# The low-rank product inside the mixer's first block, both gate turns ahead of the third output unit, three plain units first in the output's second half

## The chip, the cores and the metric

The kernel runs on one core of a Trainium2 chip. The metric is the device time of one execution in microseconds (us); several runs are taken and the median counts. Beside them one execution was profiled, which gives the span, the trace and the page of the profile.

## The reference

One encoder layer on 256 tokens of width 2048, in float32:

```python
x = x + 0.5 * swiglu(rms_norm(x, ffn1_norm), ffn1_w_gate, ffn1_w_up, ffn1_w_down)
h = rms_norm(x, mix_norm)
u, q, k, v, g, a_lr = split(h @ w_in)              # pool 1024 | q 512 | k 512 | v 1024 | gate 1024 | low rank 16
y_pool = pool_mixer(u, pool_w, pool_scale)          # trailing means over 2/4/8/16 frames, per-group map
log_a = log_sigmoid(a_lr @ gla_w_a2 + gla_b_a) / 16 # diagonal forget gate of the linear attention
y_gla = gated_linear_attention(q, k, v, log_a) * silu(g)   # 4 heads, chunks of 64 frames, per-head norm
x = x + concat(y_pool, y_gla) @ w_out
x = x + cross_attention(rms_norm(x, xattn_norm), rms_norm(mem, mem_norm))   # 256 memory tokens
x = x + 0.5 * swiglu(rms_norm(x, ffn2_norm), ffn2_w_gate, ffn2_w_up, ffn2_w_down)
out = rms_norm(x, final_norm)
```

The change concerns the projection `w_in` with the low-rank forget gate, the output gate, and the product with `w_out`.

## The kernel before

Every weight is streamed from memory once, in units of 1 MB: two 128-row slices of the weight by 1024 columns. A float32 product is made of three products of a reduced format. Each operand is split into a high part and a low part; high times high, high times low and low times high are added in PSUM. So each unit of raw weights is first split: ScalarE copies it to `wh` (the high part, L1671) and VectorE subtracts to get `wl` (the low part, L453).

A **plain** unit is 24 matmuls of 128x512 (L362). Some units go by a scheme of Strassen's kind and are called **sevens** here (L507): 7 products in place of 8, so 21 matmuls, for which VectorE forms sums of the weights (`T`, L486), and three weight blocks are split unsummed (`xh` L279, `xl` L280), the four sums as `wh` (L489) and `wl` (L453). The activations of a seven need sums as well (`Sums.make`, L424 to L436, and the `ye` tiles).

PSUM holds four tiles of two banks each. A block of eight units (`block_s`) uses two tiles (the **whole** tiles) for all units, and two more (the **parts** tiles) from its first seven on. After its last seven, `combine` (L581 to L586) reads the parts tiles, and after its last unit `join` (L596) or the residual (L767, L779) reads the whole tiles.

The order of the work comes from three things. `Stream` is a list of units and of small operations that are hung behind them: `st.op(f, n)` puts `f` behind the n-th unit that follows. When unit u is reached, the split of unit u+2 is written down first, then the matmuls of u, and the load of a further unit is issued into one of three raw buffers. If the next entry of the list is marked as a clump, the split of the low part is shared: GpSimd takes 768 of its 2048 columns (L457). A planner then orders each engine's queue by that program order and by its own estimate of when things are ready. Two means pin the order: `issue_after` puts instructions of one engine behind a named one in its queue, and `in_turn` and `among_weights` chain the splits of the weights (and the sums of activations) on VectorE and ScalarE in the order in which they were written down.

The mixer runs these blocks of eight units, each over the same activations `xs`, in the order of `ORDER_IN = (0, 2, 4, 1, 5, 3, 6, 7)` with units 1 and 3 as sevens:

- the **q/k block** (columns from 2·NB), whose rows are turned to columns by `turn_qk(1)` and `turn_qk(0)` (transposes at L789, copies at L1145);
- the **low-rank unit** (`load_a`, `a_unit`, `split_a`; L1056, L1065, L1072): one load of 16 columns, 16 matmuls into `pa`, read by `ev_a` (L1081 to L1083), which makes `aT`;
- the **pool block** (columns from 0). Inside its first unit, between its two halves, `decay_logits` (L1088 to L1096) multiplies `aT` with `wa2`; two units in, `decay` (L1096 to L1126) makes the cumulative sums of the forget gate, with three loads of activation tables. `decay` pins its logarithm behind the splits already written down, and pins the split that follows behind its subtraction (L1114);
- the **value block** and the **gate block**, with the attention of the four heads and the small pool product (L1044) between their units.

`gate(1)` and `gate(0)` turn the scaled gate rows by eight transposes each (L789), multiply them into the heads' outputs (L1253) and split them into `ys` (L285, L286). They are hung behind the first unit of the output block.

The **output block** is `into_x(w_out)` with the plan `MIXED`: its first half (1024 columns) takes the units in the order (1, 2, 3, 6, 0, 5, 4, 7) with 0 and 4 as sevens, its second half in the order (1, 2, 0, 3, 4, 5, 6, 7) with 0, 4 and 6 as sevens. `MIXED.after = (1, 4, 9)` says behind how many units of the block the sums of the activation pairs 0, 4 and 6 are made. `behind` pins the whole third unit (index 2) of the first half behind the transposes of `gate(1)` in TensorE's queue. Each half ends in four residual updates and two folds: `fold` transposes the new x (`px`, L800, 16 transposes for both) and scales it into `xs` (ScalarE L248, VectorE L240), which frees the two PSUM tiles of `px`. The query block of the cross attention follows.

Of the kernel before, what the change touches and what calls it, by code (L numbers as in the profile page):

```python
# [20 lines left out]
NB = 512  # L21
# [78 lines left out]
def build(ctx, tc, I, out):  # L100
    nc = tc.nc
    st = Stream()
# [87 lines left out]
    xs = main.tile([P, KT, 2, S], F32R, tag="xs", name="xs")  # L190
# [74 lines left out]
    def behind_weights(f):  # L265

        with tc.issue_after(latest["vector"].ins), tc.issue_after(latest["scalar"].ins):
            return f()
# [366 lines left out]
    def wload(dst, w, k0, n, n0, cols=NB):  # L635
        nc.sync.dma_start(
            dst, w[k0 * P : (k0 + n) * P, n0 : n0 + cols].rearrange("(k p) n -> p k n", p=P)
        )
# [9 lines left out]
    def wwide(w, n0, k0=0, nk=KT):  # L648

        def src(k):  # L650
            def load(raw):
                raw = raw.rearrange("p (k n) -> p k n", n=2 * NB)
                if len(loaded) < 3:
                    for kk in range(2):
                        parts = (0, NB) if not loaded else (0,)
                        for c in parts:
                            n = 2 * NB // len(parts)
                            wload(raw[:, kk : kk + 1, c : c + n], w, k + kk, 1, n0 + c, n)
                else:
                    wload(raw, w, k, 2, n0, 2 * NB)  # L660
                next(first_loads, None)
                loaded.append(1)
            return load
        return [src(k0 + k) for k in range(0, nk, 2)]
# [146 lines left out]
    class IntoX:  # L811
# [7 lines left out]
        def make_sums(self, after=None):  # L819
            for g, n in zip(self.sums.pairs, after or self.after):  # L820
# [1 line left out]

    WHOLE = IntoX((0, 4), (2, 5), ((1, 2, 3, 5, 0, 6, 4, 7), (1, 2, 0, 3, 4, 5, 6, 7)),
                  ((0, 4), (0, 4)))
    MIXED = IntoX((0, 4, 6), (1, 4, 9), ((1, 2, 3, 6, 0, 5, 4, 7), (1, 2, 0, 3, 4, 5, 6, 7)),
                  ((0, 4), (0, 4, 6)), room=3, folds=(1, 1, 2, 2))
    OUTPUT = IntoX((0, 4, 6), (0, 4, 9), ((1, 2, 3, 5, 0, 6, 4, 7), (1, 2, 0, 3, 4, 5, 6, 7)),
                   ((0, 4), (0, 4, 6)), room=3, folds=(1, 1, 2, 2))
# [3 lines left out]
    def into_x(w, act, scale, gain=None, k0=0, nk=KT, spread_too=True, src=None, way=OUTPUT,  # L832
               spread_at=3, behind=None):

        for b in range(2):
            st.op(lambda b=b: fetch_x(b, src), 2)
            cols = wwide(w, b * 2 * NB, k0, nk)
            if way.sevens[b]:
                block_s(cols, act, way.sums, way.orders[b], residual(scale, b, 0),
                        early_parts(scale, b), way.sevens[b], behind=None if b else behind)  # L840
            else:
                block_t(cols, act, residual(scale, b))
            if gain is not None:
                for j in range(2):
                    st.op(lambda c=2 * b + j: fold(c, gain), way.folds[2 * b + j])
        if gain is not None:
            st.op(lambda: finish_norm(4, spread_too), way.folds[3] + 1)
            if spread_too:
                st.op(spread_norm, spread_at)
# [94 lines left out]
    def in_ys(i):  # L944
        t = ys[:, 2 * i : 2 * i + 2].rearrange("p k a s -> p (k a s)")
        return t.rearrange("p (a n s) -> p a n s", a=2, n=4)

    qk_sums = Sums("qe", xs, (1, 3), False, 2, {0: in_ys(6), 1: in_ys(7)})
# [16 lines left out]
    w_in = I["w_in"][0]  # L965
    mix = {}
# [172 lines left out]
    def turn_qk(j):  # L1139
        if "kq" not in mix:  # L1140
            mt("kq", [P, 4 * LINES])
        t = mix["k" if j else "q"] = mix["kq"][:, j * H * S : (j + 1) * H * S].rearrange(
            "p (h s) -> p h s", h=H
        )
        nc.scalar.copy(t, rows_turned(mix["rows", j]))  # L1145
# [29 lines left out]
    def queries(h):  # L1175
        q, E, F = mix["q"][:, h, :], mix["E"], mix["F"]
        e = lambda c: E[:, 4 * h + c : 4 * h + c + 1]
        f = lambda i: F[:, i, h : h + 1]
        QD = mix["QD", h] = m4()
        at = QD_AT  # L1180
        factors = {(0, 1): e(1), (0, 2): f(0), (0, 3): f(2), (1, 2): e(2), (1, 3): f(1), (2, 3): e(3)}
        for j in range(3):
            nc.scalar.copy(QD[:, at[j] + j * CH : at[j] + (j + 1) * CH], q[:, j * CH : (j + 1) * CH])
            for c in range(j + 1, 4):
                nc.vector.tensor_scalar_mul(
                    QD[:, at[j] + c * CH : at[j] + (c + 1) * CH], q[:, c * CH : (c + 1) * CH],
                    factors[j, c],
                )

    def scores(h):  # L1190
        q, kd, QD, at = mix["q"][:, h, :], mix["k"][:, h, :], mix["QD", h], QD_AT
        ps = ptile(uid("pq"))
        for j in range(4):
            part = slice((j % 2) * CH, (j % 2 + 1) * CH)
            rhs = QD[:, at[j] + j * CH : at[j] + S] if j < 3 else q[:, 3 * CH :]
            nc.tensor.matmul(
                ps[part, j // 2, j * CH : S], kd[:, j * CH : (j + 1) * CH], rhs, start=True, stop=True
            )
        s = score_tile(h)
        for j in range(4):  # L1200
            part = slice((j % 2) * CH, (j % 2 + 1) * CH)
            nc.scalar.copy(s[part, j // 2, j * CH :], ps[part, j // 2, j * CH : S])
# [56 lines left out]

    ORDER_IN = (0, 2, 4, 1, 5, 3, 6, 7)  # L1260
    st.op(query_rows, 3)
    block_s(wwide(w_in, 2 * NB), xs, qk_sums, ORDER_IN, ev_qk, home=wide_home)
    st.op(lambda: turn_qk(1), 1)
    st.op(lambda: turn_qk(0), 2)
    st.unit(load_a, a_unit, split_a)
    st.op(ev_a)
    st.op(decay, 2)
    def head(h):
        attend(h)
# [2 lines left out]
    def scores_of(*hs):  # L1272
        for h in hs:
            st.op(lambda h=h: scores(h))

    def queries_of(*hs):
        for h in hs:
            st.op(lambda h=h: behind_weights(lambda: queries(h)))

    block_s(wwide(w_in, 0), xs, qk_sums, ORDER_IN, ev_pool, home=wide_home,  # L1280
            behind={0: (0, decay_logits)}, amid={4: lambda: queries_of(0, 1), 6: lambda: scores_of(0, 1)})
    for f, h, after in (
        (queries, 2, 1), (scores, 2, 1), (queries, 3, 1), (scores, 3, 1), (lambda _: turn_pool(), None, 2),
        (means, 1, 3), (means, 2, 4), (means, 3, 7), (means, 0, 8),
# [23 lines left out]
    def homes(of):  # L1308
        return lambda: scope.update(shared={tag: list(of[tag]) for tag in of})
# [27 lines left out]
    def mem_fold(c):  # L1337

        v = four(ptile(uid("tm")))
        for j in range(4):  # L1340
# [6 lines left out]

    MIXED.make_sums()
    into_x(I["w_out"][0], ys, 1.0, G_X, spread_too=False, way=MIXED,
           behind={2: (1, lambda: mix["turned", 1])})  # L1350
    st.op(homes(Q_HOMES))
    st.op(mem_in, 2)
    for c in range(4):
# [337 lines left out]
def program(shapes):  # L1691
    import concourse.bacc as _bacc

    nc = _bacc.Bacc("TRN2", target_bir_lowering=False, num_devices=1)
    args = {
        name: nc.dram_tensor(f"in_{name}", shapes[name], F32, kind="ExternalInput").ap()
        for name in _INS
    }
    out = nc.dram_tensor("out", _OUT, F32, kind="ExternalOutput").ap()
    with tile.TileContext(nc, schedule_with_timeline_sim=True) as tc, ExitStack() as ctx:  # L1700
        build(ctx, tc, args, out)
    return nc
# [10 lines left out]
```

## Time and profile before

| | |
|---|---|
| median of 3 runs | 2077.58 us (2077.37 to 2078.93) |
| the profiled execution's own time | 2078.92 us |
| its span | 2077.1 us (the other 1.8 us lie around the span) |
| TensorE (PE) busy, matmuls | 2061.7 us (99%) |
| VectorE (DVE) busy | 1838.8 us (89%) |
| ScalarE (ACT) busy | 1171.3 us (56%) |
| granted TensorE clock | 0.999 |
| moved by the DMA engines | 435.92 MB, mean 210 GB/s |

In the trace the q/k block's last unit begins at about 747 us, the low-rank unit at 752.8, the pool block at 756.4, the output block at 906.2 and its second half at about 951; the query block follows at about 997. A row of the timeline has the start, the duration, the engine, the line, what is written from what, how often, and in brackets the idle time of the engine before it with what ended it.

### The profile page before, as it was taken

What the parts mean: (1) busy time and instruction counts of PE and PEld (TensorE: products, weight loads), DVE (VectorE), ACT (ScalarE), POOL (GpSimd) and SP (SyncE); (2) the same over time, 40 slices, a digit from 0 to 9 for tenths busy, and PEclk for the clock granted to TensorE, in tenths of its full rate; (3) what the DMA queues carried; (4) which work ended last, traced back from release to release, by engine and by line L of the source; (5) the groups of instructions that cost most, each with busy time, mean ns of one, the idle gap of its engine ahead of it and who ended that gap; (6) DMA issues with size and microseconds to landing.
All of it is one profiled execution on the core that took longest, in us unless ns stands there. A gap on an engine that the chain in (4) does not pass through costs nothing.

```text
span 2077.1 us, 24042 instructions
## 1 busy us (share of the span) xinstructions
PE 2061.7 (99%) x9461; PEld 1713.8 (83%) x9461; DVE 1838.8 (89%) x1717; ACT 1171.3 (56%) x1190; POOL 107.5 (5%) x95
## 2 busy tenths in 40 slices
PE   9999999999999999999999999999999999999998
PEld 7888888888888887887888888888888888888886
DVE  6998899989998769889889878889988999889987
ACT  7665455554554656566755554556554555545554
POOL 0000000000000000000000000000000010000001
PEclk9999999999999999999999999999999999999999
DMA  7666766566666655457755455666576765776664
GB/s 264 203 202 223 243 210 217 184 229 235 226 198 222 234 175 183 164 197 227 266 183 196 166 183 182 203 213 216 178 243 213 236 210 192 224 241 223 207 226 155
DMA packets 122985, 435.92 MB, mean 210 GB/s; under 512 B 9844, under 2 KB 13528, under 8 KB 122488
## 3 DMA queue, kind: packets, MB, share of 16 engines
q1 hardware_dynamic: 122696, 433.86, 62.4%
q8 instruction: 74, 1.21, 0.2%
q10 hardware_dynamic: 176, 0.53, 0.1%
q14 instruction: 39, 0.32, 0.0%
HBM read 417.58 MB, written 16.78 MB: 209 GB/s over the span
## 4 chain that ended last, share of the span: by engine, by line
PE 97%; DVE 1%; ACT 1%; DMA 0%; issue 0%; SPq 0%; DVEq 0%; ACTq 0%
PE pt L362 63%; PE pt L507 29%; PE ph L789 1%; PE pl L1396 1%; PE pv L1433 1%; DVE wl L453 1%; PE px L800 0%; DMA x<-in_x 0%; PE pp L1044 0%; PE pe L362 0%; DVE T L486 0%; ACT wh L489 0%; PE pa L1072 0%; PE tm L1342 0%; PE po L1209 0%
## 5 line engine op out<-in xcount | busy, mean ns | idle before, releaser
L362 PE MATMUL pt<-wh,xs 128*128 128x512 f32 x2464 | 790.2, 391 | 0.2 <-ACT wh L279 0.2
L1671 ACT CAST wh<-raw 128x2048 fp32r<-128x2048 f32 x243 | 463.8, 1913 | 224.7 <-PE pt L362 123.7
L453 DVE TENSOR_TENSOR wl<-raw,wh 128x2048 fp32r<-128x2048 f32 (+1 forms) x243 | 516.6, 2134 | 83.1 <-ACT wh L1671 82.8
L362 PEld LDWEIGHTS pt<-wh,xs 128*128 128x128 f32 x2464 | 461.8, 188 | 95.8 <-ACT wh L279 0.6
L489 ACT CAST wh<-T 128x1024 fp32r<-128x1024 f32 x262 | 274.8, 1053 | 380.4 <-DVE T L486 367.5
L362 PE MATMUL pt<-wl,xs 128*128 128x512 f32 x1232 | 480.8, 391 | 0.7 <-DVE wl L453 0.7
L362 PE MATMUL pt<-wh,ys 128*128 128x512 f32 x1440 | 455.3, 389 | 0.0
L362 PEld LDWEIGHTS pt<-wh,ys 128*128 128x128 f32 x1440 | 270.2, 188 | 55.7
L453 DVE TENSOR_TENSOR wl<-T,wh 128x2048 fp32r<-128x2048 f32 (+1 forms) x131 | 294.4, 2247 | 8.0 <-ACT wh L489 7.6
L362 PE MATMUL pt<-wl,ys 128*128 128x512 f32 x720 | 280.9, 390 | 2.1 <-DVE wl L453 2.1
L362 PEld LDWEIGHTS pt<-wl,xs 128*128 128x128 f32 x1232 | 231.4, 188 | 48.2 <-DVE wl L453 1.1
L280 DVE TENSOR_TENSOR xl<-raw,xh 128x1536 fp32r<-128x1536 f32 x131 | 229.4, 1751 | 19.5 <-ACT xh L279 19.4
L279 ACT CAST xh<-raw 128x1536 fp32r<-128x1536 f32 x131 | 193.9, 1480 | 67.3 <-PE pt L507 43.1
L486 DVE TENSOR_TENSOR T<-T,raw 128x512 f32<-128x512 f32 x262 | 180.8, 690 | 6.7
L457 POOL TENSOR_TENSOR wl<-raw,wh 128x768 fp32r<-128x768 f32 x46 | 85.7, 1863 | 1469.4 <-DVE wl L453 1446.6
L362 PEld LDWEIGHTS pt<-wl,ys 128*128 128x128 f32 x720 | 135.2, 188 | 30.4 <-DVE wl L453 2.6
L486 DVE TENSOR_TENSOR T<-raw 128x1024 f32<-128x1024 f32 x131 | 159.5, 1218 | 0.5
L507 PE MATMUL pt<-wh,xs 128*128 128x512 f32 x392 | 152.3, 389 | 0.0
L507 PE MATMUL pt<-xh,xs 128*128 128x512 f32 x408 | 151.9, 389 | 0.0
L507 PE MATMUL pt<-wh,xe 128*128 128x512 f32 x320 | 124.3, 389 | 0.0
L507 PEld LDWEIGHTS pt<-xh,xs 128*128 128x128 f32 x408 | 76.6, 188 | 15.9
L507 PEld LDWEIGHTS pt<-wh,xs 128*128 128x128 f32 x392 | 73.6, 188 | 15.2
(270 smaller groups left out, 2073.2 us busy)
## 6 DMA issues: line engine op xcount, KB each, us to landing
raw<-in_ffn_w_down SPq DMA_DIRECT2D x88, 1024.0 KB, 5.6
raw<-in_ffn_w_up SPq DMA_DIRECT2D x80, 1024.0 KB, 5.1
raw<-in_ffn_w_gate SPq DMA_DIRECT2D x77, 1024.0 KB, 5.1
raw<-in_w_in SPq DMA_DIRECT2D x32, 1024.0 KB, 5.1
raw<-in_xattn_w_kv SPq DMA_DIRECT2D x32, 1024.0 KB, 5.0
raw<-in_w_out SPq DMA_DIRECT2D x16, 1024.0 KB, 5.9
raw<-in_xattn_w_q SPq DMA_DIRECT2D x16, 1024.0 KB, 5.7
raw<-in_xattn_w_o SPq DMA_DIRECT2D x16, 1024.0 KB, 5.7
```

The costliest lines, as they stand in the source:

```text
L279: in_turn("scalar", lambda: nc.scalar.copy(hi, src))
L280: in_turn("vector", lambda: nc.vector.tensor_tensor(out=lo, in0=src, in1=f32(hi), op=ALU.subtract))
L362: nc.tensor.matmul(ps, a, w, start=first and i == 0, stop=last and i == 2)
L453: in_turn("vector", lambda: nc.vector.tensor_tensor(out=lo[:, :n], in0=src[:, :n], in1=f32(hi[:, :n]), op=ALU.subtract))
L457: rest = nc.gpsimd.tensor_tensor(out=lo[:, n:], in0=src[:, n:], in1=f32(hi[:, n:]), op=ALU.subtract)
L486: in_turn("vector", lambda: nc.vector.tensor_tensor(out=o, in0=a, in1=b, op=ALU.add))
L489: in_turn("scalar", lambda: nc.scalar.copy(th[:, c], t[:, c]))
L507: nc.tensor.matmul(banks[n], x, w, start=n in fresh and j == 0, stop=n in ends and j == 2)
L789: rows["turned"] = nc.tensor.transpose(v[:, i, h * P : (h + 1) * P], g[:, h, i * P : (i + 1) * P], ident)
L1396: nc.tensor.matmul(ps[:, t, :M], ys[:, 4 * h + d, a, tok], xa["K", h][:, d, b, :], start=i == 0, stop=i == 11,)
L1433: nc.tensor.matmul(ps[:, d, :S], xa["V", h][:, m, a, col], xa["PT", h][:, m, b, :], start=i == 0, stop=i == 5,)
L1671: in_turn("scalar", lambda: nc.scalar.copy(hi, raw))
```

## The change

Three edits, all of them to the order of work; no instruction of the computation is added or dropped.

First, the low-rank unit, which stood behind the q/k block's last unit (7), is put between its units 6 and 7, with `ev_a` right behind it. What is hung behind "the next unit" at the end of the block therefore now counts units of the pool block alone: `turn_qk(1)` follows the pool block's first unit and `turn_qk(0)` its second. `decay` stays behind the pool block's second unit.

Second, in `MIXED` the second half's order becomes (1, 2, 3, 0, 4, 5, 6, 7), so that the plain unit 3 comes ahead of the seven 0, and the seven 0 is followed directly by the seven 4; the sums of activation pair 6 are made behind the eleventh unit in place of the ninth.

Third, the third unit of the output block's first half is pinned behind the transposes of `gate(0)` in place of those of `gate(1)`. Since `gate(1)` is written down ahead of `gate(0)`, that pins it behind both where the planner keeps their order.

```diff
-    MIXED = IntoX((0, 4, 6), (1, 4, 9), ((1, 2, 3, 6, 0, 5, 4, 7), (1, 2, 0, 3, 4, 5, 6, 7)),
+    MIXED = IntoX((0, 4, 6), (1, 4, 11), ((1, 2, 3, 6, 0, 5, 4, 7), (1, 2, 3, 0, 4, 5, 6, 7)),
                   ((0, 4), (0, 4, 6)), room=3, folds=(1, 1, 2, 2))
...
     st.op(query_rows, 3)
-    block_s(wwide(w_in, 2 * NB), xs, qk_sums, ORDER_IN, ev_qk, home=wide_home)
+    def low_rank():
+        st.unit(load_a, a_unit, split_a)
+        st.op(ev_a)
+
+    block_s(wwide(w_in, 2 * NB), xs, qk_sums, ORDER_IN, ev_qk, home=wide_home, amid={6: low_rank})
     st.op(lambda: turn_qk(1), 1)
     st.op(lambda: turn_qk(0), 2)
-    st.unit(load_a, a_unit, split_a)
-    st.op(ev_a)
     st.op(decay, 2)
...
     into_x(I["w_out"][0], ys, 1.0, G_X, spread_too=False, way=MIXED,
-           behind={2: (1, lambda: mix["turned", 1])})
+           behind={2: (1, lambda: mix["turned", 0])})
```

More of the change, by code (lines that the diff above doesn't have):

```diff
@@ L1280, in build @@
     block_s(wwide(w_in, 0), xs, qk_sums, ORDER_IN, ev_pool, home=wide_home,
-            behind={0: (0, decay_logits)}, amid={4: lambda: queries_of(0, 1), 6: lambda: scores_of(0, 1)})
+            behind={0: (0, decay_logits)},
+            amid={4: lambda: queries_of(0, 1), 6: lambda: scores_of(0, 1)})
     for f, h, after in (
```

## The prediction

> **What bounds the kernel now.** I read the page first: its engines and its chain.
>
> ```profile
> PE 2061.7 (99%) x9461; PEld 1713.8 (83%) x9461; DVE 1838.8 (89%) x1717; ACT 1171.3 (56%) x1190; POOL 107.5 (5%) x95
> PE 97%; DVE 1%; ACT 1%; DMA 0%; issue 0%; SPq 0%; DVEq 0%; ACTq 0%
> ```
>
> TensorE is the kernel. The three edits neither add nor drop a matmul, so what they can give is its idle time alone. The waits of TensorE show how little that is, and the timeline shows where it lies:
>
> ```profile
> PE pt L362 <- DVE wl L453: 2.8, 2, 2.1
> PE pt L507 <- DVE xl L280: 0.7, 2, 0.5
> ...
> 782.77 0.50 PE L362 MATMUL pt<-wl,xs 128*128 128x512 f32 x1 [0.70 <-DVE wl L453]
> ...
> 941.59 0.50 PE L507 MATMUL pt<-xl,ys 128*128 128x512 f32 x1 [0.53 <-DVE xl L280]
> ...
> 966.15 0.39 PE L362 MATMUL pt<-wh,ys 128*128 128x512 f32 x1
> 968.67 0.50 PE L362 MATMUL pt<-wl,ys 128*128 128x512 f32 x1 [2.14 <-DVE wl L453]
> ...
> 1065.70 0.50 PE L507 MATMUL pt<-xl,xs 128*128 128x512 f32 x1 [0.19 <-DVE xl L280]
> 957.06 5.44 PE pt L362 x24
> 962.50 1.36 PE pt L507 x6
> ```
>
> The two rows of waits (total, times, longest) hold four stops, 3.5 us in all, each ended by VectorE. Three lie in the stretch that the change touches: at 782 (pool block), 941 (output block, first half) and 966 (second half); the fourth, at 1065, is in the query block behind it. The last two rows are of the chain of waits; the first of them gives the pace: 24 matmuls in 5.44 us, 0.227 each. By it the stop at 966 costs 968.67 - 966.15 - 0.227 = 2.29 us, 0.15 more than the 2.14 of idle time, since the pipeline starts anew. With 0.15 for each, the stops are worth 0.85, 0.68, 2.29 and 0.34 us. The three in reach make 3.82 us, all four 4.16. That is the ceiling: 4.16 us of 2077.58 is 0.2%, and 0.2% is also about what a measurement of this kernel can tell from no change.
>
> **Edit 1, the low-rank unit one unit earlier.** What makes the stop at 782 stands in the chain of waits, piece by piece (start, duration, what):
>
> ```profile
> 754.96 1.59 PE pa L1072 x7
> ...
> 762.91 1.92 PE pz L1088 x8
> 764.83 2.98 PE pt L362 x12
> ...
> 767.88 1.99 ACT wh L489 x2
> ...
> 769.89 1.28 ACT L1096
> ...
> 771.18 1.06 ACT m L1096
> ...
> 773.17 1.28 ACT L1102
> ...
> 776.82 2.45 DVE m L1107 x4
> ...
> 780.43 2.29 DVE wl L453
> ```
>
> The low part at 780.43 belongs to the pool block's fifth unit. The code pins it behind the subtraction of the decay, that behind the scans (L1107), and those wait for the logarithm (L1102; its table load is the piece at 773.17), which is pinned behind the high parts of the seven ahead (L489 at 767.88). These wait for a `wh` buffer, which the pool block's first unit frees at its end, and this unit's second half is written behind the product `pz`. `pz` needs `aT`, the output of the low-rank unit. Now that unit runs directly ahead of the pool block, so the planner lets 24 matmuls go first and `pz` starts 6.4 us after the end of the low-rank unit (754.96 + 1.59 = 756.55), where the block begins. With `aT` ready a whole unit earlier (24 matmuls, 5.44 us), `pz` can follow the first half, 12 matmuls or 2.72 us in: at 759.3 in the clock of these rows. It ends at 761.2, the first unit 12 matmuls later at 763.9 in place of 764.83 + 2.98 = 767.8, and the chain behind it, unchanged in its pieces, moves by 3.9 us: the low part ends at 780.43 + 2.29 - 3.9 = 778.8. TensorE wants it at 782.77 - 0.85 = 781.9. The stop goes, with 3.1 us to spare: 0.85 us.
>
> The rows have the table loads at 1.28 us, with the next activation 0.01 later (769.89 + 1.28, then 771.18). The Trainium skill (ScalarE: Activation LUTs, "What ACT_TABLE_LOAD costs") puts a switch at 1.28 us plus a drain of 1.38. The trace here shows no such drain; with it, as an estimate from that page, the two switches on this chain would take 2.8 us more and the spare time would shrink to 0.3 us, the sum staying as it is.
>
> What is moved along: the load of the 16 columns now goes ahead of unit 7's weights on the queue, and the split of unit 7 no longer stands next to a clump, so GpSimd's share of it falls to VectorE.
>
> ```profile
> 749.04 1.49 DVE L453 TENSOR_TENSOR wl<-raw,wh 128x1280 fp32r<-128x1280 f32 x1
> ...
> 754.94 2.29 DVE L453 TENSOR_TENSOR wl<-raw,wh 128x2048 fp32r<-128x2048 f32 x1 [0.77 <-ACT wh L1671]
> raw<-in_w_in SPq DMA_DIRECT2D x1, 128.0 KB, 3.0
> 741.00:757.00 16.00, 16.00 (x75) 13.28 (x74) 10.59 (x10) 7.71 (x10) 3.32 (x4) 1.00 0.59 205
> ```
>
> One share fewer is 2.29 - 1.49 = 0.8 us more on VectorE, in a stretch in which it is busy 10.59 of 16 us (third engine in the window's row, behind PE and PEld); I put it at nothing. Without that cover it would cost 0.8. The small load lands in 3.0 us, and unit 7's weights are wanted 3.6 us later than now (16 matmuls run first), so the swap pays for itself; if not, the bound is 3.0 us once. `turn_qk` comes later by up to a unit; its copies are wanted only by the multiplication behind the scans. Zero.
>
> **Edit 3, both gates turned first.** Rows of TensorE, ScalarE and VectorE around the gates:
>
> ```profile
> 917.09 1.03 PE L789 MATMUL ph<-ident,rows 128*128 128x128 f32 x8
> 921.76 0.93 PE L789 MATMUL ph<-ident,rows 128*128 128x128 f32 x7
> 914.91 2.52 ACT L1244 ACTIVATE rows<-rows,r 128x256 f32<-128x256 f32 x6
> 922.73 1.66 DVE L1253 SCALAR_TENSOR_TENSOR t<-m,gains,ph 128x256 f32<-128x256 f32 x4 [1.50 <-PE ph L789]
> ```
>
> `gate(0)`'s transposes end 4.6 us behind `gate(1)`'s (922.69 against 918.12), and VectorE stands 1.50 us for them. From 922.73 on it hardly rests again: what it does next decides the stops at 941 and 966. With both sets in a row (1.0 us each) the second ends at about 919.1, before VectorE is through with the first (1.66 us of products, from 918.1 on), so the 1.50 us of idle time go and its queue runs 1.5 us earlier. The stop at 941 waits for a part on this queue and is 0.68 long: it goes. The new wait is TensorE's: 24 matmuls of the third unit, and all units behind it, now queue behind `gate(0)`. Its rows are scaled at 914.91 + 2.52 = 917.43, the second set would start at about 918.1: 0.7 us to spare. Zero; if ScalarE puts more work ahead of the scaling, a high part of the two-piece kind above (1.99 us), it is 1.3 us.
>
> **Edit 2, three plain units first.** The rows of the second half:
>
> ```profile
> 963.71 1.91 PE L800 MATMUL px<-ident,x 128*128 128x128 f32 x16
> ...
> 962.23 2.28 DVE L453 TENSOR_TENSOR wl<-T,wh 128x2048 fp32r<-128x2048 f32 x1
> 964.43 0.68 DVE L424 TENSOR_TENSOR j<-ys 128x512 f32<-128x512 f32 x1
> ...
> 966.34 2.28 DVE L453 TENSOR_TENSOR wl<-raw,wh 128x2048 fp32r<-128x2048 f32 x1
> ...
> 971.05 2.04 DVE L240 SCALAR_TENSOR_TENSOR xs<-px,gains,xs 128x256 fp32r<-128x256 f32 x5
> ...
> 979.01 2.28 DVE L453 TENSOR_TENSOR wl<-raw,wh 128x2048 fp32r<-128x2048 f32 x1
> 981.95 0.39 PE L362 MATMUL pt<-wl,ys 128*128 128x512 f32 x1
> L280 DVE TENSOR_TENSOR xl<-raw,xh 128x1536 fp32r<-128x1536 f32 x131 | 229.4, 1751 | 19.5 <-ACT xh L279 19.4
> L486 DVE TENSOR_TENSOR T<-T,raw 128x512 f32<-128x512 f32 x262 | 180.8, 690 | 6.7
> L486 DVE TENSOR_TENSOR T<-raw 128x1024 f32<-128x1024 f32 x131 | 159.5, 1218 | 0.5
> 946.00:985.00 39.00, 36.86 (x171) 30.44 (x170) 37.51 (x40) 22.54 (x32) 0.00 (x0) 1.00 0.72 235
> ```
>
> At 966 TensorE wants the low part of plain unit 3, which VectorE makes at 966.34, behind the weight sums and splits of the seven 0 (to 964.51) and the sums for pair 6 (from 964.43, 1.9 us). After the edit both stand behind unit 3, so its low part is there some 8 us sooner and this stop goes. What is late next is the pair of sevens in a row. A seven keeps VectorE for 6.6 us (by the three rows of the page's groups, 1.22 + 2 x 0.69 for `T` and 1.75 for `xl`, and 2.28 for `wl`) and TensorE for 21 x 0.227 = 4.76. VectorE's work up to the low part of unit 5 is the same in both orders and nearly without a gap; it ends now at 979.01 + 2.28 = 981.29, and 1.5 us earlier with edit 3: 979.8. TensorE comes to the matmul that needs it at 981.95 now, and without the two stops would at 981.95 - 0.68 - 2.29 = 978.98. So about 0.8 us of the 2.29 comes back as a stop at units 4 and 5. The bounds are zero, if the planner puts the eight evictions of `px` (2.04 us for five in the row at 971.05, so 3.3) behind that low part, and the whole 2.29 and more, below.
>
> **The sum.** 0.85 + 0.68 + 2.29 - 0.8 = 3.0 us off. The profiled execution took 2078.92 (a span of 2077.1 and 1.8 around it), 1.3 above the median of the runs, so it would go to 2075.9, and the median from 2077.58 to 2074.6.
>
> **Rivals.** *The stop only moves* (15 in 100). VectorE was busy 37.51 of 39 us from 946 to 985 (the last row above), and two sevens in a row need 13.2 us of it against 9.5 of TensorE. If edit 3's 1.5 us are lost again to a weight that lands late or a late scaling, edit 2 gives nothing and only the 0.85 remains, with or without the 0.68: 2076.7 or 2076.0. For it speaks VectorE's load, against it that the sums of pair 6 leave the place where they hurt.
>
> *Everything goes* (10 in 100): no stop at units 4 and 5, and the one at 1065 goes with VectorE's earlier queue: 4.16 us or a little more by the restarts of smaller gaps, 2073.3.
>
> *PSUM holds the sevens back: slower* (14 in 100 by over 0.2%, 8 in 100 by less). `px` takes two tiles and the whole tiles two; the seven 0 needs two more, for 12 of its 21 matmuls. Now they are freed by the evictions that end at 971.05 + 2.04 = 973.1, and the plain unit 3 fills the wait. After the change a seven follows, which needs the same tiles. The seven 0 would start at about 969.0 (`px` starts at 963.71, behind the six matmuls of the seven at 962.50 that will come later, so at 963.71 - 1.36 - 0.68 = 961.7; then 1.9 us of transposes and a unit of 5.44) and has 9 matmuls, 2.0 us, that need no parts tile. If VectorE's queue has the evictions behind the seven 4's splits, they end at about 979, TensorE stands from 971.0 to 979, 8.0 us, and the sum is 8.0 - 3.8 = 4.2 us slower: 2081.8. It decides against the change from evictions that end later than 971.0 + 3.8 = 974.8. Against it: the folds are written down ahead of those splits, and the plain unit now stands where the evictions run; by the rows they would end near 973.1 - 1.5 (edit 3) - 1.9 (the sums for pair 6, moved behind) = 969.7.
>
> That nothing else can fill such a hole shows at the stop at 966: the next matmul lacked its low part, the one behind it needs only the high part, which TensorE had just used at 966.15, and yet TensorE stood until 968.67. The Trainium skill (PSUM — Partial Sum Buffer, "Engine vs sequencer instructions") has the rule: matmuls start and complete in program order. The trace agrees with its 2.14 us of idle time. By a queue that could overtake, this rival would cost nothing.
>
> **How the numbers follow.** The forecast case, 1.5 to 4.1 us faster, has 53 in 100 and gives 2074.6. Faster by over 0.2% (4.16 us) needs every stop gone: 0.10. Slower by over 0.2% needs a new stop of 8 us: 0.14. The rest, 0.76, lies within. The range takes in the ceiling (2073.0) and the beginning of the slower rival, 2 us slower (2079.6).
>
> **What would show it.** `pz` about 3 us into the pool block and no stop there; sixteen transposes in a row at the gates, and VectorE's 1.50 gone; no stop near 941; three plain units in the second half with the evictions of `px` during the third; a remaining stop of about 0.8 us at units 4 and 5. It is wrong if a stop of several us stands ahead of the seven 0's products, or if TensorE waits for ScalarE's rows at the gates.

## The result, and the profile after

The changed kernel took 2074.72 us (median of 21 runs, 2073.96 to 2075.67) against 2078.66 for the kernel before in the same runs (21, 2076.91 to 2080.23): a ratio of 0.9982, interval 0.9975 to 0.9988. The forecast was 3.0 us off the kernel before; measured are 3.9 by the medians, 2.95 between the lowest times (2076.91 and 2073.96), and 2.5 to 5.2 by the interval (0.0012 and 0.0025 of 2078.66), which does not reach zero. The profiled execution took 2074.4 us, a span of 2072.6.

The page of the changed kernel, busy time by engine:

```profile
PE 2060.7 (99%) x9461; PEld 1714.4 (83%) x9461; DVE 1839.5 (89%) x1717; ACT 1170.5 (56%) x1190; POOL 105.8 (5%) x94
```

As many matmuls, one GpSimd instruction fewer (the share of unit 7's split, which fell to VectorE). TensorE's waits (total, times, longest):

```profile
...
PE pt L362 <- DVE wl L453: 1.2, 1, 1.2
PE px L726 <- DMA x<-in_x: 0.3, 1, 0.3
PE pt L507 <- DVE xl L280: 0.2, 1, 0.2
```

Of the four stops by VectorE, 3.5 us of idle time, two are left: a new one of 1.2 and the old one of 0.2 in the query block.

The two spans differ by 4.5 us, more than any sum of stops allows. Two landmarks part the edits from the rest: the last of the 16 transposes ahead of the mixer (its start: 1.91, the length of the row, less 0.27, that of one, so 1.64 behind the row's start), and the first score product `pl` of the cross attention. The timeline of the kernel before:

```profile
713.78 1.91 PE L800 MATMUL px<-ident,x 128*128 128x128 f32 x16
...
1148.52 0.28 PE L1396 MATMUL pl<-K,ys 128*128 128x256 f32 x1
```

and of the changed kernel:

```profile
712.17 1.91 PE L800 MATMUL px<-ident,x 128*128 128x128 f32 x16
...
1143.99 0.28 PE L1399 MATMUL pl<-K,ys 128*128 128x256 f32 x1
```

Between them lie 1148.52 - 715.42 = 433.10 us before and 1143.99 - 713.81 = 430.18 after. This **middle** holds all that was edited, and lost 2.9 us. The other 1.6 lie ahead of it, where the code is the same: the changed kernel's profile waited 0.3 us for the first load of x, the one before 1.5, which is 1.2 of it. Below, "the middle" of a run is always this stretch, taken from its own two landmarks.

The places that the prediction names, in the changed kernel's timeline of TensorE, ScalarE and VectorE:

```profile
757.58 1.99 PE L1088 MATMUL pz<-aT,wa 32*128 32x256 f32 x8
758.16 1.33 ACT L1134 ACTIVATE rows<-rows,Rcol 128x512 f32<-128x512 f32 x2
762.61 2.00 ACT L489 CAST wh<-T 128x1024 fp32r<-128x1024 f32 x2 [0.46 <-ACT m L1094]
764.52 1.05 ACT L1095 ACTIVATE m<-m 128x1024 f32<-128x1024 f32 x1
766.49 1.28 ACT L1096 ACT_TABLE_LOAD   x1
767.78 1.06 ACT L1096 ACTIVATE m<-m 128x1024 f32<-128x1024 f32 x1
776.20 2.29 DVE L453 TENSOR_TENSOR wl<-raw,wh 128x2048 fp32r<-128x2048 f32 x1
780.04 0.39 PE L362 MATMUL pt<-wl,xs 128*128 128x512 f32 x1
...
914.44 1.91 PE L789 MATMUL ph<-ident,rows 128*128 128x128 f32 x16
915.51 1.65 DVE L1253 SCALAR_TENSOR_TENSOR t<-m,gains,ph 128x256 f32<-128x256 f32 x4 [0.53 <-PE ph L789]
916.10 0.48 PE L362 MATMUL pt<-wh,ys 128*128 128x512 f32 x1
916.42 0.39 PE L362 MATMUL pt<-wl,ys 128*128 128x512 f32 x1
...
960.66 2.29 DVE L453 TENSOR_TENSOR wl<-T,wh 128x2048 fp32r<-128x2048 f32 x1 [0.25 <-ACT wh L489]
964.68 1.66 DVE L240 SCALAR_TENSOR_TENSOR xs<-px,gains,xs 128x256 fp32r<-128x256 f32 x4 [0.47 <-ACT xs L248]
966.86 1.65 DVE L240 SCALAR_TENSOR_TENSOR xs<-px,gains,xs 128x256 fp32r<-128x256 f32 x4
972.90 0.68 DVE L424 TENSOR_TENSOR j<-ys 128x512 f32<-128x512 f32 x1
975.01 2.28 DVE L453 TENSOR_TENSOR wl<-raw,wh 128x2048 fp32r<-128x2048 f32 x1
975.67 0.50 PE L507 MATMUL pt<-xh,ys 128*128 128x512 f32 x1
977.35 0.50 PE L362 MATMUL pt<-wl,ys 128*128 128x512 f32 x1 [1.17 <-DVE wl L453]
977.68 0.63 PE L362 MATMUL pt<-wh,ys 128*128 128x512 f32 x2
```

`pz` stands inside the first unit, the low part of the pool block's fifth unit is there (778.49) before TensorE wants it (780.04), the gates are sixteen transposes in a row, and nothing stops at the places of 941 and 966. One stop stands at unit 5 of the output's second half: VectorE makes its low part at 975.01, behind the sums for pair 6 (from 972.90).

### The profile page after: what moved, and what is told of

Read it like the earlier page. It is cut to its first block, busy times and chain, and to the rows that moved or that the text cites. A ratio compares the mean times of both kernels' runs of the same rounds, so it can differ in the third digit from the quotient of the medians.

```text
span 2072.6 us, 24047 instructions
## 1 busy us (share of the span) xinstructions
PE 2060.7 (99%) x9461; PEld 1714.4 (83%) x9461; DVE 1839.5 (89%) x1717; ACT 1170.5 (56%) x1190; POOL 105.8 (5%) x94
## 4 chain that ended last, share of the span: by engine, by line
PE 98%; DVE 1%; DMA 0%; ACT 0%; issue 0%; SPq 0%; DVEq 0%; ACTq 0%
PE pt L362 64%; PE pt L507 29%; PE ph L789 2%; PE pl L1399 1%; PE pv L1436 1%; PE px L800 0%; DVE wl L453 0%; PE pp L1044 0%; PE pe L362 0%; DMA x<-in_x 0%; PE pa L1072 0%; PE tm L1345 0%; PE po L1209 0%; PE px L726 0%; PE pq L1196 0%; DVE xs L240 0%
```

## The experiments

**Which edit gives what.** My theory: each edit is worth its own stop, and edit 2 gives part of its stop back. The rivals: the edits do nothing and runs just differ, or one edit carries all. First the kernel before, unchanged, for what two profiles of one kernel differ by.

> The kernel before, unchanged, once more. It tells how much of the difference between the two profiles is no work of the change: 1.6 us of their 4.5 us lie ahead of the mixer, 1.2 of it in one wait for the first load of x (1.5 us before, 0.3 after). If that wait varies from execution to execution, this profile shows another value of it than 1.5, the four stops at 782, 941, 966 and 1065 stand as they were (0.70, 0.53, 2.14, 0.19 us of idle time), and the time is within 0.05% of the kernel before. If the wait belongs to the program, it stands at 1.5 again.

2078.19 against 2077.87 us, ratio 1.0002 (0.9993 to 1.0011); the middle took 432.98, 0.12 from the other profile. Its waits of TensorE:

```profile
PE pt L362 <- DVE wl L453: 2.7, 2, 2.0
...
PE pt L507 <- DVE xl L280: 0.7, 2, 0.5
```

The same four stops and no wait for x at all; its span was 2075.3. So two spans of one kernel differ by 1.8 us, 1.6 of it ahead of the first landmark (712.14 against 713.78), and the middle is the finer measure.

Then each edit by itself. Edit 1 alone is the changed kernel with these two lines as before:

```diff
-    MIXED = IntoX(... (1, 4, 11), (... (1, 2, 3, 0, 4, 5, 6, 7)),
+    MIXED = IntoX(... (1, 4, 9), (... (1, 2, 0, 3, 4, 5, 6, 7)),
-           behind={2: (1, lambda: mix["turned", 0])})
+           behind={2: (1, lambda: mix["turned", 1])})
```

> Edit 1 alone. By the theory that each edit takes away the stop that was put down to it: pz about 2.8 us into the pool block, no stop there, the stops at the output block unchanged (0.53 and 2.14 of idle time), 0.85 to 1.1 us faster than the kernel before. By the rival that the gain comes from VectorE's queue as a whole running earlier, the later stops shrink too and it is more than 1.5 us faster.

2077.22 us, ratio 0.9997 (0.9989 to 1.0006); middle 432.30, 0.7 to 0.8 off. The stop in the pool block is gone, and the stretch up to the gates' first transposes lost 1.03 us (915.71 - 713.43 against 917.09 - 713.78). 0.31 came back at the stop of 966, here 2.45 us of idle time in place of 2.14. Its timeline, backwards from the matmul:

```profile
967.58 0.50 PE L362 MATMUL pt<-wl,ys 128*128 128x512 f32 x1 [2.45 <-DVE wl L453]
...
948.65 2.29 DVE L453 TENSOR_TENSOR wl<-raw,wh 128x2048 fp32r<-128x2048 f32 x1 [1.29 <-ACT wh L1674]
...
946.70 1.91 ACT L1674 CAST wh<-raw 128x2048 fp32r<-128x2048 f32 x1 [2.01 <-DMA raw<-in_w_out]
```

VectorE stood 1.29 us for a high part whose weights had landed late. In the kernel before it stood 1.01 us at the same place (949.75), so 0.28 us of this is new; its full queue carried that to unit 3's low part, 19 us later. In the three profiles without edits 2 and 3 the two move together: 0.91 us here and 2.03 at unit 3 in the repetition, 1.01 and 2.14 in the kernel before, 1.29 and 2.45 in this one.

Edit 2 alone is the kernel before with the one line:

```diff
-    MIXED = IntoX(... (1, 4, 9), (... (1, 2, 0, 3, 4, 5, 6, 7)),
+    MIXED = IntoX(... (1, 4, 11), (... (1, 2, 3, 0, 4, 5, 6, 7)),
```

> Edit 2 alone: the new order of the second half, without the earlier gates. By the theory that VectorE's work up to the low part of unit 5 bounds the second half: the stop at 782 and that at 941 stand, the one ahead of unit 3 goes and comes back at unit 5 at 1.6 to 2.4 us, so 0 to 0.7 us faster. By the rival that the order itself is what helps, the stop at unit 5 is no longer than the 1.2 us of idle time of the changed kernel, and it is 0.8 to 1.1 us faster.

2076.98 us, ratio 0.9997 (0.9989 to 1.0006); middle 432.34, 0.7 off. The stop at 966 went, and this one came at unit 5. With its restart it is 1.45 us, where 1.6 at the least was expected if VectorE's work bounds the half:

```profile
979.49 0.50 PE L362 MATMUL pt<-wl,ys 128*128 128x512 f32 x1 [1.18 <-DVE wl L453]
```

Edit 3 alone:

```diff
-           behind={2: (1, lambda: mix["turned", 1])})
+           behind={2: (1, lambda: mix["turned", 0])})
```

> Edit 3 alone: both gates turned ahead of the third output unit, the old order of the second half. By the theory that VectorE's queue runs 1.5 us earlier by it: sixteen transposes in a row, VectorE's wait of 1.50 us for them gone, the stop at 941 gone (0.68 us), and the stop ahead of unit 3 shrinks from 2.3 by the other 0.8 us to about 1.5: 1.5 us faster. By the rival that the stop at 966 has nothing to do with the gates, it stands at 2.1 of idle time and the gain is 0.7 us.

2076.30 us, ratio 0.9995 (0.9986 to 1.0004); middle 431.37, 1.7 off, the most of the three. The stop at 941 is gone, and the one at 966 shorter:

```profile
965.57 0.50 PE L362 MATMUL pt<-wl,ys 128*128 128x512 f32 x1 [1.54 <-DVE wl L453]
```

By the middles the three give 0.75 + 0.7 + 1.7 = 3.1 apart and 2.9 together: nearly a sum. None can be told from no change by its ratio alone, so this rests on one profile of each edit, and on the 0.12 us by which two profiles of one kernel differed.

**What is missing without one of them.** Edits 1 and 2 without 3, and edits 1 and 3 without 2, which are the changed kernel with the gates' line, or the `MIXED` line, as before.

> The change without edit 3 (edits 1 and 2). Measured from the last transposes ahead of the mixer to the first score product of the cross attention, the kernel before took 433.1 us, the changed one 430.2, edit 1 alone 0.7 less than before, edit 2 alone 0.7 less, edit 3 alone 1.6 less. If the edits add up, this is 431.6 to 431.8: VectorE's wait of 1.50 at the gates and the stop of 0.66 near 941 are back, the stop at unit 5 of the second half is 1.45. If edit 3 only pays together with edit 2, it is above 432.

2076.49 us, ratio 0.9990 (0.9982 to 0.9999); middle 431.41, 0.2 below what a sum of the edits gives. The stop of 941 is there again, and the one at unit 5 is as long as in the changed kernel:

```profile
939.07 0.50 PE L507 MATMUL pt<-xl,ys 128*128 128x512 f32 x1 [0.52 <-DVE xl L280]
...
976.29 2.29 DVE L453 TENSOR_TENSOR wl<-raw,wh 128x2048 fp32r<-128x2048 f32 x1
978.64 0.50 PE L362 MATMUL pt<-wl,ys 128*128 128x512 f32 x1 [1.17 <-DVE wl L453]
```

On top of edits 1 and 2, edit 3 gives 431.41 - 430.18 = 1.2 us.

> The change without edit 2 (edits 1 and 3, old order of the second half). If the edits add up, 430.7 to 430.9 in the same measure. By the theory that edits 2 and 3 serve the same stop, little is left for edit 2 once the gates are early: 430.3 to 430.5, with a stop ahead of unit 3 of about 1.7 where the changed kernel has 1.45 at unit 5.

2075.33 us, ratio 0.9985 (0.9976 to 0.9994); middle 430.55. The timeline at unit 3:

```profile
960.42 0.69 DVE L424 TENSOR_TENSOR j<-ys 128x512 f32<-128x512 f32 x1
...
962.33 2.29 DVE L453 TENSOR_TENSOR wl<-raw,wh 128x2048 fp32r<-128x2048 f32 x1
964.67 0.50 PE L362 MATMUL pt<-wl,ys 128*128 128x512 f32 x1 [1.69 <-DVE wl L453]
```

With edits 1 and 3 in place, edit 2 gives only 430.55 - 430.18 = 0.4 us: it takes one stop out and puts another in. Both stops have the same sums (from L424 on; 1.9 us here, 2.1 in the changed kernel) right ahead of the low part that TensorE wants. That suggests a rival to the order of units: the place of the sums is what counts.

**The sums one place later.** The changed kernel with

```diff
-    MIXED = IntoX((0, 4, 6), (1, 4, 11), ...
+    MIXED = IntoX((0, 4, 6), (1, 4, 12), ...
```

> The changed kernel with the sums of pair 6 behind the twelfth unit in place of the eleventh, so that the low part of unit 5 goes ahead of them in VectorE's queue. By the theory that the remaining stop (1.45 us at unit 5) is VectorE's queue and that the 2.1 us of the sums stand in it, the stop at unit 5 goes; since the seven 6 still needs all of VectorE's work, 0.7 to 1.1 us of it come back there: 0.3 to 0.7 us faster than the changed kernel, 429.5 to 429.9 in the same measure. By the rival that the stop is due to the evictions of px, it stays and nothing changes.

2074.07 us, ratio 0.9979 (0.9970 to 0.9988); middle 429.32, 0.9 below the changed kernel. The timeline:

```profile
973.18 2.29 DVE L453 TENSOR_TENSOR wl<-raw,wh 128x2048 fp32r<-128x2048 f32 x1
975.39 0.69 DVE L424 TENSOR_TENSOR j<-ys 128x512 f32<-128x512 f32 x1
...
982.24 0.50 PE L507 MATMUL pt<-xl,ys 128*128 128x512 f32 x1 [0.34 <-DVE xl L280]
```

The low part of unit 5 comes ahead of the sums and nothing stops there; 0.34 turn up at the seven 6, which the sums now delay.

**Less work for VectorE.** If its queue is the bound, handing parts of splits to GpSimd must help as well. In the changed kernel, the low parts that are split at the start of units 1, 2 and 3 of the second half are shared:

```diff
-                shared = done == until and self.clump_behind(at)
+                shared = (done == until and self.clump_behind(at)) or done in self.shares
...
+            if way is MIXED and b:
+                st.shares.update(len(st.units) + i for i in (1, 2, 3))
```

> The changed kernel with GpSimd taking 768 of 2048 columns of three low parts in the second half (units 2, 3 and the seven 0). That takes 3 x 0.8 = 2.4 us off VectorE ahead of unit 5's low part. By the theory that VectorE's queue is the bound, the stop of 1.45 goes and the one at the query block shrinks: 428.5 to 429.0 in the same measure, 1.2 to 1.7 us faster than the changed kernel. By the rival that the two engines hinder each other at the memory, VectorE's instructions beside GpSimd's get longer than 2.28 (or 1.22, 0.69 for the sums) and the gain is under 0.5 us.

2074.28 us, ratio 0.9979 (0.9970 to 0.9987); middle 429.48, 0.7 below the changed kernel where at least 1.2 was expected. The stop at unit 5 halves, from 1.45 to 0.76 us. The timeline tells why it did not go (GpSimd and VectorE; the lines count one or two more here):

```profile
947.92 1.85 POOL L458 TENSOR_TENSOR wl<-raw,wh 128x768 fp32r<-128x768 f32 x1 [60.36 <-DVE wl L454]
953.32 1.21 DVE L487 TENSOR_TENSOR T<-raw 128x1024 f32<-128x1024 f32 x1
953.53 2.72 POOL L458 TENSOR_TENSOR wl<-raw,wh 128x768 fp32r<-128x768 f32 x1 [3.75 <-DVE wl L454]
961.81 1.83 POOL L458 TENSOR_TENSOR wl<-T,wh 128x768 fp32r<-128x768 f32 x1 [5.57 <-DVE wl L454]
963.68 1.23 DVE L487 TENSOR_TENSOR T<-raw 128x1024 f32<-128x1024 f32 x1 [1.94 <-POOL wl L458]
```

The third share is of the seven 0, read from `T`. GpSimd holds that buffer until 963.64, and VectorE, which wants it for the next seven, stands 1.94 us. The two other shares did what they were to do: the weight sums at 953.32 come 1.55 us sooner behind the first landmark than in the changed kernel (953.32 - 713.11 against 953.93 - 712.17), two times 0.8.

**Both, without the third share.** Sums at 12 and shares at `(1, 2)`, beside the changed kernel once more.

> The changed kernel, unchanged, beside the next three on the same chip: the same stop of 1.45 us at unit 5, 430.0 to 430.4 us between the landmarks, and another value of the wait at the start than 0.3. It gives the time that the others are held against.

2075.42 against 2078.38 us, ratio 0.9983 (0.9974 to 0.9992); middle 430.23, 0.05 from the first profile, and this time 1.6 us of wait for x.

> The sums of pair 6 behind the twelfth unit, and GpSimd's share for the low parts of units 2 and 3 of the second half alone (not for the seven 0, whose share held back the buffer of the next weight sums by 1.9 us). By the theory that VectorE's queue is the bound, 1.6 us less on it takes away the last 0.50 of stop at the seven 6: 428.6 to 428.9 between the landmarks, 0.5 us faster than with the sums alone and 1.4 faster than the changed kernel. By the rival that waits for buffers and for ScalarE eat what VectorE is spared, it stays at 429.1 to 429.4.

2073.17 us, ratio 0.9971 (0.9959 to 0.9982); middle 428.47. Of TensorE's waits one is left behind the start, that of the query block:

```profile
PE pt L508 <- DVE xl L281: 0.2, 1, 0.2
```

The window of that half has its length, the busy time of PE, PEld, VectorE, ScalarE and GpSimd with the number of their instructions, the granted clock, and the DMA engines' share and GB/s:

```profile
942.00:981.00 39.00, 39.00 (x182) 32.55 (x181) 37.34 (x42) 23.73 (x32) 4.58 (x2) 1.00 0.75 249
```

No stop is left in the mixer and the output: TensorE was busy 39.00 of 39 us. This version is the fastest of all, ahead of both kernels: 2.2 us below the changed one in the same comparison, its slowest run (2074.38) ahead of that one's fastest (2074.46), and 1.8 in the middle.

**Order or sums?** The square is closed by the new order with the old place of the sums, and the old order with the new one, both with edits 1 and 3.

```diff
-    MIXED = IntoX((0, 4, 6), (1, 4, 11), (... (1, 2, 3, 0, 4, 5, 6, 7)),
+    MIXED = IntoX((0, 4, 6), (1, 4, 9), (... (1, 2, 3, 0, 4, 5, 6, 7)),    # new order, old sums
+    MIXED = IntoX((0, 4, 6), (1, 4, 11), (... (1, 2, 0, 3, 4, 5, 6, 7)),   # old order, new sums
```

> The changed kernel with the sums of pair 6 behind the ninth unit again, the new order kept. By the theory that only VectorE's work ahead of unit 5's low part counts and not its order, the stop at unit 5 stays at 1.2 to 1.6 us (the sums stand ahead of the seven 0's split, which has 2 us to spare): 429.9 to 430.5 between the landmarks. By the rival that the place of the sums was the useful part of edit 2, a stop of about 1 us or more appears at the seven 0 beside the one at unit 5, and it is above 430.8.

2074.69 us, ratio 0.9981 (0.9972 to 0.9990); middle 430.14. The timeline of TensorE in the two sevens:

```profile
970.59 0.47 PE L507 MATMUL pt<-wh,ys 128*128 128x512 f32 x1 [0.33 <-DVE xs L240]
...
972.76 0.50 PE L507 MATMUL pt<-xl,ys 128*128 128x512 f32 x1 [0.32 <-DVE xl L280]
```

Here a seven waits for the evictions of `px` (L240): the PSUM rival exists, at 0.33 us. The time is as expected and its place is not: nothing stops at unit 5, whose low part now has no sums right ahead of it; two short stops stand in the sevens instead.

> The changed kernel with the old order of the second half (the seven 0 ahead of unit 3), the sums of pair 6 behind the eleventh unit. The sums leave the place ahead of unit 3's low part, so that comes 2 us sooner and the stop there (1.85 us in the kernel without edit 2) goes or shrinks to under 0.4. By the theory that VectorE's total ahead of unit 5 counts, 1 us or more of it comes back at the seven 4 or unit 5: 430.0 to 430.6. By the rival that the old order with later sums would have done better than the new order, it is below 429.8.

2073.58 us, ratio 0.9976 (0.9967 to 0.9986); middle 429.06. Its timeline of VectorE, and TensorE at unit 5:

```profile
960.41 2.29 DVE L453 TENSOR_TENSOR wl<-raw,wh 128x2048 fp32r<-128x2048 f32 x1
...
974.07 2.28 DVE L453 TENSOR_TENSOR wl<-raw,wh 128x2048 fp32r<-128x2048 f32 x1
976.41 0.50 PE L362 MATMUL pt<-wl,ys 128*128 128x512 f32 x1 [0.22 <-DVE wl L453]
```

| middle, with edits 1 and 3 | sums at 9 | sums at 11 | sums at 12 |
|---|---|---|---|
| old order (0 ahead of 3) | 430.55 | 429.06 | not run |
| new order (3 ahead of 0) | 430.14 | 430.18 | 429.32 |

The rival is right about what counts. Either half of edit 2 takes the stop at unit 3 away by itself; they differ in what comes back. In the old order the later sums give 1.5 us: unit 3's low part follows the seven 0's directly (960.41), and 0.22 us of idle time comes back at unit 5. The new order with the old sums gives 0.4, and once the sums are late it costs 1.1: at unit 5 TensorE stands 1.17 us again in place of 0.22. Of this 1.1, some 0.6 are waits of VectorE: the changed kernel has two (0.25 and 0.47 in its rows above) that this one has not, and this one stands 0.1 longer near 945. The rest I have not traced instruction by instruction; where the fold stands in the two orders is told below.

## Why the prediction was right, and where it was not

**The time.** 3.0 us were forecast and 2.9 found in the middle; the median differs by 3.9 in the first comparison and 3.0 in the repetition (2078.38 to 2075.42). "Within 0.2%" held for the median (0.18%, with an interval of 0.12 to 0.25), and by the ceiling: no stop outside those four was touched.

**Edit 1** was sized 0.85 and gave 1.04 by the gates' first transposes (914.44 - 712.17 against 917.09 - 713.78). `pz` started at 757.58, about three us into the pool block, as forecast, and the chain behind it moved. Its spare time was not 3.1 but 780.04 - 776.20 - 2.29 = 1.55 us, for the chain moved by 780.43 - 776.20 less 1.6 of the start, 2.6 and not 3.9. The pieces did not stay as they were: ScalarE put row scalings of the q/k rows (L1134, from 758.16) ahead of the decay's first step, and so its second (L1095, 1.05 us), which had run ahead of the high parts, now runs behind them at 764.52, in the chain. The drain that the Trainium skill (ScalarE: Activation LUTs, "What ACT_TABLE_LOAD costs") adds to a switch does not show here either: the load at 766.49 takes 1.28 us, and the next activation starts 0.01 later, at 767.78.

**Edit 3** went as worked out: sixteen transposes in a row, VectorE's 1.50 us gone, the stop at 941 gone, no wait for ScalarE's rows. (The 0.53 us at 915.51 are ahead of the first set; the kernel before had them too, at 918.16.) Alone it gave 1.7 and not 0.68, since an earlier queue also shortened the stop at 966 (2.14 to 1.54 of idle time), beside the small gains told below. In the sum that part is edit 2's anyway; on top of edits 1 and 2 it gave 1.2.

**Edit 2** is the term that was mis-sized: a stop of 0.8 was forecast at units 4 and 5, and 977.35 - 975.67 - 0.227 = 1.45 us stood there. VectorE's side came out: the forecast had its low part ready at 979.8, and the trace has 975.01 + 2.28 = 977.29, which is 979.9 in the clock of before (2.65 later there: 1.6 at the start, 1.04 of edit 1). TensorE's side failed: wanted at 978.98 by the forecast, at 975.67 + 0.227 + 2.65 = 978.55 in the trace. It came 0.4 us sooner, since each stop removed is worth more than its idle time and 0.15: the matmul behind the restart is slow by another 0.10 (977.68 - 977.35 - 0.227 = 0.10 in the row above), and each break of the matmuls by transposes, one at the gates in place of three, costs 0.09 (916.42 - 916.10 - 0.227). These small gains, some 0.5 in all (2.9 less 0.85 + 0.68 + 2.29 - 1.45), and the 0.65 that came back too much make up for each other. That the sum fits to 0.1 is in part luck.

VectorE's 979.9 is in part luck as well. The forecast let edit 3's 1.5 us shorten this stop, from 981.29 - (981.95 - 2.29) = 1.63 to 0.8. In the runs it is as long without edit 3 as with it, 1.17 us of idle time each. What holds VectorE is the fold. In the changed kernel ScalarE waits 0.45 us for TensorE's transposes `px`, which start at 962.01, and VectorE 0.47 us for ScalarE (964.68 above). In the repetition VectorE came later, since it had stood 1.15 us near 945 in place of 0.90; it waited at the fold 0.26 us less, and the stop stayed at 1.18. ScalarE's row of the changed kernel, and VectorE's of the repetition:

```profile
963.08 3.03 ACT L248 ACTIVATE xs<-px,gains 128x256 fp32r<-128x256 f32 x8 [0.45 <-PE px L800]
...
965.95 1.66 DVE L240 SCALAR_TENSOR_TENSOR xs<-px,gains,xs 128x256 fp32r<-128x256 f32 x4 [0.21 <-ACT xs L248]
```

From the start of `px` VectorE's low part takes 977.29 - 962.01 = 15.3 us, and TensorE is at the matmul that wants it after 975.67 + 0.227 - 962.01 = 13.9. The difference of 1.4 is the stop, whatever VectorE had gained before. So the step that failed is "nearly without a gap", with the 1.5 us carried over it: the lead from the gates ends at the fold. (Without edit 3 VectorE comes to the fold with no lead and no wait.) In this order only work between the fold and unit 5 counts, which is why the sums one place later ended this stop. In the old order with the late sums `px` starts at 960.18, 15.8 us ahead of the same matmul's turn, and VectorE waits for ScalarE nowhere behind it.

Its reason was incomplete too. The prediction removed the stop at 966 by putting both the seven 0 and the sums behind unit 3; the square shows that either is enough, that the late sums alone give 1.5, and that the order gives 0.4 without them and takes 1.1 with them. Both were in the same line of the diff, and the prediction did not price them apart.

**The rivals.** *The stop only moves*: true of 1.45 of the 2.29 us, not of all. *Everything goes*: false for the changed kernel, though the last version does it up to the query block. There its premise fails: the stop at 1065 did not yield to VectorE's earlier queue in any run. It stayed at 0.35 us even where VectorE stood just ahead of it, as the timeline with the sums at 12 shows:

```profile
1058.84 1.76 DVE L280 TENSOR_TENSOR xl<-raw,xh 128x1536 fp32r<-128x1536 f32 x1 [4.14 <-ACT xh L279]
1060.65 0.50 PE L507 MATMUL pt<-xl,xs 128*128 128x512 f32 x1 [0.19 <-DVE xl L280]
```

VectorE waited 4.14 us for ScalarE's high part; its load is not the cause. *PSUM holds the sevens back*: the evictions ended at 966.86 + 1.65 = 968.51, or 971.2 in the clock of before, against 969.7 forecast and 974.8 at which it would have decided. They did not run during the third plain unit alone, as the prediction's sign had it: the seven 0's products begin at 965.58, while they run. Still no product waited for them in the changed kernel, and 0.33 us showed where the sums stood early.

Open is why the medians of the first comparison differ by 1 us more than the middles. The lowest times differ by 2.95, so the runs of the kernel before spread further above their lowest; a weight that lands late and goes straight to the stop at 966, as in the profile of edit 1 alone, would do that, but no run separates it from the wait at the start. Against it stands that edit 2 alone, without a stop at 966, spreads as wide (2076.10 to 2079.94).

## What to carry to other kernels

Where one engine's pinned queue feeds the bottleneck, look at what stands directly ahead of the piece that is wanted next: moving 2.1 us of sums one place gave 0.9 us, more than the new order of units by itself (0.4). A lead that this engine gains earlier ends where it waits for something that the bottleneck itself makes, as at the fold here. Then take load off that queue, but not from a buffer that it needs back at once. And where an effect is smaller than the difference between two executions, measure between two landmarks around the edit: the middles of one kernel agreed to 0.12 us, the spans only to 1.8.

## What the runs showed of the hardware

The wait for the very first load varied from 0 to 1.6 us between executions of the same kernel (none, 1.5; and 0.3, 1.6 above).

The same subtraction of 768 columns took GpSimd 1.85 us, and 2.72 where VectorE was at a sum of two SBUF operands when it began (`T`, 953.32 to 954.53, not itself longer than elsewhere); the last version has the same pair, with 2.71. The Trainium skill (SBUF — State Buffer, "Who interferes with whom") says that such a VectorE instruction and a GpSimd one that reads SBUF exclude each other, and that the later one blocks. The trace agrees: 954.53 - 953.53 = 1.0 us of overlap, and 0.87 us longer.
